# Hybrid decoder layer: attention scores, GLA products and the gate product on plain float32, softmax for eight heads at once, x kept for the first units

## The chip, the cores and the metric

The kernel runs on one core of one Trainium2 chip. The metric is device time in microseconds (us) of one execution; the time before is the median of three runs. The engines of the core are PE (TensorE), DVE (VectorE), ACT (ScalarE), POOL (GpSimd) and SP (SyncE, which here only issues DMAs).

## The reference

One layer for 2048 prompt tokens and 8 x 8 decode tokens, model width 1024, all in float32. One projection of x gives the inputs of two branches, a sliding-window attention (8 heads of width 64 on 2 KV heads, window 128, learned sink per head, relative bias) and a gated linear attention (GLA, 4 heads, key width 128, value width 256, a recurrent state). Both are gated, projected, merged, projected again and layer-normalised with the residual:

```python
z = einsum('btd,dn->btn', x, w_in)
q, k, v, g_att, gq, gk, gv, g_gla, g_lr, r_att, r_gla = split(z)
s = einsum(q, k) * HEAD_DIM**-0.5 + rel_bias          # 128 queries x 256 keys per block
m = max(max(s), sink); p = exp(s - m)
o_att = einsum(p / (sum(p) + exp(sink - m)), v)
log_a = log_sigmoid(g_lr @ w_gk_up + b_gk) / 16       # the gate product, rank 16
# GLA, chunk by chunk, b = cumsum(log_a):
o = einsum(q*exp(b), S) + einsum(tril(einsum(q*exp(b), k*exp(-b))), v)
S = exp(b_last) * S + einsum(k*exp(b_last - b), v)
h_att = (o_att * silu(g_att)) @ w_pa; h_gla = (norm(o) * silu(g_gla)) @ w_pg
y = (sigmoid(r_att) * h_att + sigmoid(r_gla) * h_gla) @ w_o
x = layer_norm(ALPHA * x + y)
```

Outputs are the new x for both kinds of tokens, the last window of keys and values, and the GLA states.

## The kernel before

**Projections.** All large products go through eight passes (lines 298 to 304): one over the attention columns (5 column groups), three over the GLA columns, then w_pa, the two merge gates and w_pg (4 groups each). A pass uses a seven-product scheme for 2 x 2 blocks (Strassen's kind: 7 block products, `ORDER` at line 51, instead of 8). A **unit** is one of the seven products for one of three token stretches (`s`, two times 352 tokens each); a **group** is one unit for one column group of 128 output rows. Each group is, for each of four 128-row slices of the contraction, three matmuls of 128 x 128 by 128 x 352 on `float32r` operands (lines 1160 to 1162): every float32 operand is split into a high part (a copy to `float32r`, made by ACT in line 144) and a low part (the difference, made by DVE or POOL in line 145), and high x high, low x high and high x low are summed in PSUM. `split` does both. DVE adds the products up (lines 236 to 253), and finished columns go to DRAM.

**Order of the work.** PE's instructions are issued in the order written; the other engines' instructions are ordered by the scheduler of the framework, within each engine first in, first out on the chip. Between two groups the main loop calls `tick()`, which runs what has been hung up with `at(t, fn)` for that tick. So attention, GLA, the set-up of masks and biases and the block combinations all run as side work between projection groups, at hand-set ticks (one tick is one group). Transfers of SP's queue go in order too: loads of x for a unit are issued two or three units ahead (lines 1140 to 1142).

**Start.** The first unit loads its quarter of x in four pieces; every further unit of products 1, 2 and 3 loads its own 704 KB from x (`raw_x`, line 204). For products 7, 6, 5 and 4, sums of blocks of x are needed: `xload` and `xcombo` (lines 501 to 526) load all of x again, in twelve jobs at ticks 1 to 25, compute the low-rank gate input with small matmuls (line 512), form the sums on DVE (lines 371 to 374) and store them in `xc_d`. The gate input is stored as high and low part (`gl_d`, 64 rows).

**Attention** (lines 536 to 645) works on eight stretches of 256 tokens, two blocks of 128 queries in each, five ticks per block (`SB = 5`, line 768). Keys are loaded twice per KV head into both halves of the partitions and split (line 569); queries are split into the halves of two tiles, `qa` and `qb` (lines 582 to 585), so that one matmul with 128 rows of contraction covers both parts. A call of `att_scores` treats one KV head: for each of four heads two `float32r` matmuls of 256 columns (lines 598, 599), bias added by DVE (line 600), maximum (603), four exponentials on ACT with their sums (606), small steps on 4 columns (604, 607 to 610), four scalings on DVE (612). `att_trans` transposes the probabilities on PE (line 623), four and five ticks after the scores; `att_out` multiplies with the values on float32 operands (line 639).

**GLA** (lines 796 to 1061) takes each head's 2048 prompt tokens in steps of 128, in chunks of 256 tokens, with the 64 decode tokens at the end of the last chunk. Steps stand `ST` ticks apart, about 4.9 by the formula at its end; the four heads follow each other. Per chunk: the gate product (line 856, on 96 rows: both parts of the operands stacked), log-sigmoid, cumulated sums, exponentials, and the products with q and k (`gla_kq`, with a split of the query). Per step: `gla_v` (two transposes, a split of the values), `gla_a` (the score product on float32 at line 916, a transpose of the keys at 917, the causal mask, splits of both), `gla_b` (three times `mm3`, three `float32r` products of 256 columns each, lines 938 to 940; the state update at 957, the state's split; a norm on ACT and POOL) and `gla_c` (two transposes at 967, the gating product on DVE). `samp_a` and `samp_b` do the same for the decode tokens.

**End.** After the last pass come the w_o product (lines 1205 to 1207 and 1216 to 1219) and the layer norm.

Of the kernel before, what the change touches and what calls it, by code (L numbers as in the profile page):

```python
# [29 lines left out]
G = 4  # L30
# [25 lines left out]
def kernel(ctx, tc, io):  # L56
# [63 lines left out]
    gl_d = dram.tile([64, NT], F32, name="gl_d")  # L120
# [185 lines left out]
    units = [(q, i, s) for q in passes for i in ORDER for s in range(MS)]  # L306
# [14 lines left out]
    for n in range(0, len(units), MS):  # L321
        q, i, _ = units[n]
        for p in range(q.np):
            plan[max(n - MS + MS * p // q.np, -1)].append((n, q, i, p))
    raws, wts, xs, xp, parts = {}, {}, {}, {}, {}

    def issue_w(n):
        for u, q, i, p in plan.get(n, []):
            raws[u, p] = q.raw_w(i, p)

    def make_w(n):
        for u, q, i, p in plan.get(n, []):
            wts[u, p] = q.prep_w(i, p, raws.pop((u, p)))

    def issue_x(n):
        if n < len(units) and n not in xs and n not in xp:
# [8 lines left out]
    def issue_parts(g):  # L345
        if g < len(groups) and g not in parts:
# [3 lines left out]
    combos = {"x": deque((xT, xc_d, 4, k, s) for s in range(MS) for k in range(4)),  # L350
              "a": deque((ua_d, ac_d, 2, k, s) for s in range(MS) for k in range(2)),
              "u": deque((None, uc_d, 4, k, s) for k0 in (0, 2) for s in range(MS) for k in (k0, k0 + 1))}

    def combine_load(job):
# [7 lines left out]
        x1 = mt("xk", 2 * T, 7, name="x1") if src is xT else w4(name="x1")[:, :2 * T]  # L362
        x2 = w4(name="x2")[:, :2 * T]
# [22 lines left out]
    raws[0, 0] = q0.raw_w(1, 0)  # L386
    x0 = mtile("xb", F32, "xs")
    hl0 = [mtile("xb", F32R, n) for n in ("xh", "xl")]
    for k in range(4):
        ts = slice(k * T, (k + 1) * T)  # L390
        nc.sync.dma_start(x0[:, ts], xT[:, k, toks(0, 0)])
        if k == 0:
            wts[0, 0] = q0.prep_w(1, 0, raws.pop((0, 0)))
        split(hl0[0][:, ts], hl0[1][:, ts], x0[:, ts])
    xp[0] = hl0
    for p in range(1, 5):
        raws[0, p] = q0.raw_w(1, p)
        wts[0, p] = q0.prep_w(1, p, raws.pop((0, p)))
    plan[-1] = [e for e in plan[-1] if e[0] != 0]
    issue_x(1)  # L400
    issue_x(2)
    issue_w(-1)
    make_w(-1)
    issue_w(0)
# [5 lines left out]
    bsel = const.tile([P, NB], F32, name="bsel")  # L410
# [88 lines left out]
    cx = {}  # L499

    def xload():
        job = combos["x"].popleft()
        cx[job[4], job[3]] = combine_load(job)

    def xcombo(s, k, eng):

        x1, x2, dst, last = cx.pop((s, k))
# [6 lines left out]
        combine_do(x1, x2, dst, last, eng)  # L514
        if k == 3:
            ps = glp.pop(s)
            gh, gl = (w4(F32R, n)[:, :T] for n in ("glh", "gll"))
            split(gh, gl, ps[:, :T])
            for i, g_ in enumerate((gh, gl)):
                for j in range(4):  # L520
                    r0 = 32 * i + 16 * (j // 2)
                    nc.gpsimd.dma_start(gl_d[r0:r0 + 16, toks(s, j % 2)], g_[32 * j:32 * j + 16].bitcast(F32))
# [13 lines left out]
    def att_load(c):  # L536
# [5 lines left out]
        A["kl"], A["kd"] = ([mt("kz", W + AT, 7, F32R, n) for _ in range(2)] for n in ("kl", "kd"))  # L542
        for kv in range(2):
            for r in (slice(0, HD), slice(HD, P)):
                nc.sync.dma_start(A["kl"][kv][r, k0:].bitcast(F32),
                                  z_kv[kv * HD:(kv + 1) * HD, 0, t0 - W + k0:t0 + AT])
        A["vT"] = mt("vT", AT, 1)
        nc.sync.dma_start(A["vT"], z_kv[:, 1, t0:t0 + AT])
# [851 lines left out]
```

## Time and profile before

| | |
|---|---|
| median of three runs | 1988.36 us (1981.45 to 1990.43) |
| profiled execution | 1982.41 us |
| span of its trace | 1980.6 us |
| PE, DVE, ACT, POOL busy | 91%, 77%, 49%, 36% of the span |
| mean granted TensorE clock | 0.957 |
| DMA | 430.67 MB, mean 217 GB/s |

The profile is of one execution. A row of the groups gives line, engine, operation, out<-in, shape and count; after the bar the group's busy us, the mean ns of one, and the idle time of the engine just before them with what ended it. A row of the waits gives who waited for whom, the total us, the times, and the longest. A row of the timeline gives the start and the duration in us and, in brackets, the idle time before it; the ends of matmuls are modelled, so the step from one start to the next is the better price of a matmul. A row of the stages gives the busy us of each engine in a stretch of the span, the granted clock, the DMA share and GB/s.

### The profile page before, as it was taken

The page shows a single profiled execution, that of the slowest core. Times are in us where ns is not written, and L with a number is a line of the kernel's source. Part 1 is how long each engine was busy: PE and PEld are TensorE (multiplying, and loading weights), DVE is VectorE, ACT ScalarE, POOL GpSimd, SP SyncE. Part 2 cuts the span into 40 slices and gives each one's busy share as a digit, 9 for nine tenths or more (in the row PEclk, how much of TensorE's full clock was granted, in tenths as well). Part 3 has the DMA queues.
Part 4 walks back from the last instruction along what each step waited for, and adds up shares of the span by engine and source line. Part 5 has one row for each costly group of instructions (what it writes and reads, how often), then busy time and mean ns, then how long its engine had stood idle before and what let it go on. Part 6 is the DMA issues. An engine that isn't in the chain of part 4 may idle for free.

```text
span 1980.6 us, 31502 instructions
## 1 busy us (share of the span) xinstructions
PE 1794.6 (91%) x10771; PEld 1669.9 (84%) x10771; DVE 1532.7 (77%) x2872; ACT 978.5 (49%) x2139; POOL 716.5 (36%) x604
## 2 busy tenths in 40 slices
PE   8699997988899989889899898999988999989998
PEld 7589986867689988878898798988888999987886
DVE  5657669998996798767987878799768957866656
ACT  3143345645554655665677466676655653212100
POOL 2442153231235645545442224311445216541111
PEclk9799999999899989999999899999998999999999
DMA  9966764444556777554566787578786897797431
GB/s 352 334 226 193 224 201 161 138 142 137 180 176 184 258 249 229 170 183 147 176 193 213 233 278 233 180 246 281 252 286 228 294 327 268 237 309 243 162 118 54
DMA packets 286833, 430.67 MB, mean 217 GB/s; under 512 B 28093, under 2 KB 227573, under 8 KB 286656
## 3 DMA queue, kind: packets, MB, share of 16 engines
q1 hardware_dynamic: 284720, 426.35, 66.1%
q0 software_dynamic: 1856, 2.17, 0.4%
q8 instruction: 85, 1.39, 0.3%
q14 instruction: 76, 0.62, 0.1%
q10 hardware_dynamic: 96, 0.13, 0.0%
HBM read 306.80 MB, written 122.63 MB: 217 GB/s over the span
## 4 chain that ended last, share of the span: by engine, by line
PE 41%; DVE 25%; DMA 13%; ACT 8%; POOL 6%; issue 5%; SPq 1%; DVEq 0%; POOLq 0%; ACTq 0%
PE pd L1160 9%; PE pd L1161 9%; PE pd L1162 8%; PE pd L1207 3%; PE pd L1206 3%; PE pd L1205 3%; DVE wl L145 2%; DVE s L612 2%; ACT xh L144 2%; DVE xl L145 2%; DMA ws<-w_g 2%; DMA ws<-w_at 1%; DVE nm L603 1%; POOL a L243 1%; DVE s L600 1%
## 5 line engine op out<-in xcount | busy, mean ns | idle before, releaser
L1160 PE MATMUL pd<-xh,wh 128*128 128x352 f32 x2484 | 842.3, 339 | 39.2 <-ACT xh L144 20.7
L1161 PE MATMUL pd<-xl,wh 128*128 128x352 f32 x2484 | 817.9, 329 | 20.1 <-DVE xl L145 14.8
L1162 PE MATMUL pd<-xh,wl 128*128 128x352 f32 x2484 | 816.2, 329 | 0.0
L1160 PEld LDWEIGHTS pd<-xh,wh 128*128 128x128 f32 x2484 | 482.6, 194 | 67.7 <-issue 22.8
L1161 PEld LDWEIGHTS pd<-xl,wh 128*128 128x128 f32 x2484 | 484.1, 195 | 23.9 <-DVE xl L145 17.7
L1162 PEld LDWEIGHTS pd<-xh,wl 128*128 128x128 f32 x2484 | 482.4, 194 | 0.0
L145 POOL TENSOR_TENSOR xl<-xs,xh 128x1408 fp32r<-128x1408 f32 x63 | 207.8, 3298 | 234.0 <-ACT xh L144 227.2
L144 ACT CAST xh<-xs 128x1408 fp32r<-128x1408 f32 (+2 forms) x171 | 218.2, 1277 | 109.5 <-PE pd L1161 93.6
L145 DVE TENSOR_TENSOR wl<-ws,wh 128x512 fp32r<-128x512 f32 (+1 forms) x231 | 190.9, 835 | 71.7 <-ACT wh L144 59.5
L145 DVE TENSOR_TENSOR xl<-xs,xh 128x1408 fp32r<-128x1408 f32 (+2 forms) x108 | 170.5, 1580 | 46.7 <-ACT xh L144 45.6
L144 ACT CAST wh<-ws 128x512 fp32r<-128x512 f32 (+1 forms) x231 | 134.7, 594 | 86.3 <-PE pd L1161 53.0
L243 POOL TENSOR_TENSOR a<-a,a 128x352 f32<-128x352 f32 x99 | 108.3, 1104 | 98.9 <-DVE a L242 93.4
L931 POOL TENSOR_SCALAR sq<-sq 128x1 f32<-128x1 f32 (+1 forms) x68 | 32.3, 476 | 260.6 <-ACT ring L930 260.6
L1205 PE MATMUL pd<-woh,x 128*128 128x512 f32 x256 | 101.2, 395 | 0.7 <-ACT woh L144 0.7
L1207 PE MATMUL pd<-wol,x 128*128 128x512 f32 x256 | 101.2, 395 | 0.6 <-DVE wol L145 0.6
L1206 PE MATMUL pd<-woh,x 128*128 128x512 f32 x256 | 101.4, 396 | 0.3 <-DVE x L145 0.3
L176 POOL TENSOR_TENSOR ws<-ws 128x512 f32<-128x512 f32 (+1 forms) x32 | 41.7, 1304 | 154.0 <-DVE fin L270 27.9
L606 ACT ACTIVATE s<-s,nm 128x256 f32<-128x256 f32 (+1 forms) x128 | 62.7, 491 | 58.5 <-DVE nm L604 57.6
L144 ACT CAST x<-xst 128x384 fp32r<-128x384 f32 (+2 forms) x48 | 22.3, 486 | 139.2 <-PE pd L1206 106.4
L933 ACT ACTIVATE ring<-pa,sq 128x256 f32<-128x256 f32 (+1 forms) x68 | 32.3, 474 | 118.0 <-POOL sq L932 118.0
L178 POOL TENSOR_TENSOR ws<-ws 128x512 f32<-128x512 f32 (+1 forms) x32 | 44.3, 1384 | 88.6 <-DMA ws<-w_g 30.0
L623 PE MATMUL pa<-ident,s 128*128 128x128 f32 x248 | 44.1, 307 | 35.5 <-DVE s L612 35.3
(284 smaller groups left out, 3354.7 us busy)
## 6 DMA issues: line engine op xcount, KB each, us to landing
xs<-xc_d SPq DMA_DIRECT2D x72, 704.0 KB, 4.6
xs<-xT SPq DMA_DIRECT2D x53, 704.0 KB, 4.6
ws<-w_g SPq DMA_DIRECT2D x108, 256.0 KB, 3.7
xc<-tt_d SPq DMA_DIRECT2D x48, 352.0 KB, 5.2
ws<-w_at SPq DMA_DIRECT2D x45, 256.0 KB, 6.4
ws<-w_ra SPq DMA_DIRECT2D x36, 256.0 KB, 4.3
ws<-w_rg SPq DMA_DIRECT2D x36, 256.0 KB, 4.5
ws<-w_pg SPq DMA_DIRECT2D x36, 256.0 KB, 4.8
```

Of the source, the lines that this page charges most:

```text
L144: pin["a"] = nc.scalar.copy(dst_h, src)
L145: i = eng.tensor_tensor(dst_l, src, dst_h.bitcast(F32), ALU.subtract)
L178: tt(r[0], r[0], r[1], ALU.add)
L243: pin["p"] = nc.gpsimd.tensor_tensor(u, u, a, ALU.add)
L606: nc.scalar.activation(s[:, g, k0:], s[:, g, k0:], AF.Exp, bias=nm[:, g:g + 1], accum_out=sm[:, g:g + 1])
L623: nc.tensor.transpose(tp[:, g * P:(g + 1) * P], s[:, g, hf * W:(hf + 1) * W], ident)
L1160: mm(ps, wh[:, ks], xh[:, ts], start=(k == 0), stop=False)
L1161: mm(ps, wh[:, ks], xl[:, ts], start=False, stop=False)
L1162: mm(ps, wl[:, ks], xh[:, ts], start=False, stop=(k == q.kh - 1))
L1205: mm(ps, xh[:, xs], hi, start=(k == 0), stop=False)
L1206: mm(ps, xl[:, xs], hi, start=False, stop=False)
L1207: mm(ps, xh[:, xs], lo, start=False, stop=(k == KT - 1))
```

## The change

- **Attention.** Keys and values are loaded once per stretch, unsplit; there are no split queries. Scores are single float32 matmuls with 64 rows of contraction, the two KV heads in rows 0 to 63 and 64 to 127 of the array; the scale moves into the bias step. One call takes two heads of each KV head, and the second call then does the softmax for all eight heads, with half of the scalings on ACT. A block has seven ticks; the transposes come five and six ticks after the second score call.
- **GLA.** All products are single float32 matmuls; the splits of query, values, scores, keys and state are gone. The transpose of the keys moves from `gla_a` to `gla_v`, and one ACT copy brings values and keys out of PSUM. The gate product has 32 rows instead of 96, and the gate input is stored without a low part. Within a step of `st` ticks, `gla_v` stands at a quarter, `gla_b` at three quarters, `gla_c` at one and a half. Attention ends 32 ticks later, so `ST` becomes about 4.4.
- **Decode tokens.** The GLA products use two row halves of the array; the old states are loaded five ticks ahead by a function of their own; the attention part's outputs are written from SP's queue instead of POOL's.
- **Start.** The first six units run as products 1 and 2 of one token stretch after the other. All eight row slices of x of a stretch are loaded once and kept: the units split from them, and the block sums are formed in place. Weights for the second unit are loaded right behind those of the first; the weights of the third product are all prepared in one unit, those of the fourth in two.

```diff
-    units = [(q, i, s) for q in passes for i in ORDER for s in range(MS)]
+    units = [(passes[0], i, s) for s in range(MS) for i in ORDER[:2]]
+    units += [(passes[0], i, s) for i in ORDER[2:] for s in range(MS)]
+    units += [(q, i, s) for q in passes[1:] for i in ORDER for s in range(MS)]
...
-            plan[max(n - MS + MS * p // q.np, -1)].append((n, q, i, p))
+            if n == 3 * MS:
+                plan[n - 2 + 2 * p // q.np].append((q, i, p))
+            elif n > 2 * MS:
+                plan[n - MS + MS * p // q.np].append((q, i, p))
+            elif n == 2 * MS:
+                plan[n - 1].append((q, i, p))
...
     def make_x(n):
-        if n < len(units) and n not in xp:
+        if n < 2 * MS and n not in xp:
+            _, i, s = units[n]
+            xp[n] = [mtile("xb", F32R, m) for m in ("xh", "xl")]
+            for k in range(4):
+                split(*(t[:, k * T:(k + 1) * T] for t in xp[n]), xk[s, k][i - 1][:, :T])
+        elif n < len(units) and n not in xp:
...
+    def xload(s, k, parts_=((0, 2), (1, 2))):
+        if (s, k) not in xk:
+            xk[s, k] = mt("xk", 2 * T, 7, name="x1"), w4(name="x2")[:, :2 * T]
+        for j, m in parts_:
+            o = 0 if m else 1
+            nc.sync.dma_start(xk[s, k][j][:, o * T:max(m, 1) * T if m else 2 * T],
+                              xT[:, 4 * j + k, 2 * s * T + o * T:2 * s * T + (m or 2) * T])
...
-    for j in range(12):
-        at(1 + 1.5 * j, xload)
-        at(8 + 1.5 * j, lambda j=j: xcombo(j // 4, j % 4, nc.vector))
+    for s in range(MS):
+        for k in range(4):
+            at(10 * s + min(2 + k, 4), lambda s=s, k=k: xcombo(s, k))
...
+    def att_scores(c, bi, g0):
...
+        ps = [pa().rearrange("p (a k) -> p a k", a=2) for _ in range(2)]
+        for j in range(2):
+            for kv in range(2):
+                r = slice(kv * HD, (kv + 1) * HD)
+                mm(ps[kv][:, j, k0:], A["zq"][r, g0 + j, qs], A["kk"][r, 0, ks], start=True, stop=True,
+                   tile_position=(kv * HD, 0))
+        for kv in range(2):
+            nc.vector.scalar_tensor_tensor(A["s", bi, kv][:, g0:g0 + 2, k0:], ps[kv][:, :, k0:], HD ** -0.5,
+                                           st1["bias", kv][:, g0:g0 + 2, k0:], ALU.mult, ALU.add)
+        if g0 == 0:
+            return
...
+        for h in range(NH):
+            sl = A["s", bi, h // G][:, h % G, k0:]
+            if h % 2:
+                nc.scalar.mul(sl, sl, rd[:, h:h + 1])
+            else:
+                nc.vector.tensor_scalar(sl, sl, rd[:, h:h + 1], None, op0=ALU.mult)
...
-    SB = 5
+    SB = 7
...
+            at(o + 1, lambda c=c, bi=bi: att_scores(c, bi, 2))
+            at(o + 6, lambda c=c, bi=bi: att_trans(c, bi, 0))
+            at(o + 7, lambda c=c, bi=bi: att_trans(c, bi, 1))
+            at(o + 9, lambda c=c, bi=bi: att_out(c, bi))
...
     def gla_v(B, i):
...
-        split(gh[:n], gl[:n], v)
+        nc.tensor.transpose(tp[:n, HV:HV + HK], B["k2"][:, ts], ident)
+        nc.scalar.copy(g[:n], tp[:n, :HV + HK])
...
     def gla_b(B, i):
...
-            mm3(op[:, :HV], [t[:, ts] for t in B["qi"]], R["Ss"][S], True, False)
+            mm(op[:, :HV], B["qb"][:, ts], R["S"][S], start=True, stop=False)
         sp = pa()
-        mm3(sp[:, :HV], kT2, gv, True, True)
-        mm3(op[:, :HV], As, gv, S is None, True)
+        mm(sp[:, :HV], kT2, gv, start=True, stop=True)
+        mm(op[:, :HV], As, gv, start=(S is None), stop=True)
...
-        if not (B["last"] and i == B["nt"] - 1):
-            split(R["Ss"][Sn][0], R["Ss"][Sn][1], R["S"][Sn])
...
-                at(o + 3, lambda B=B, i=i: gla_b(B, i))
-                at(o + 7, lambda B=B, i=i: gla_c(B, i, P, i * P))
+                at(o + st / 4, lambda B=B, i=i: gla_v(B, i))
+                at(o + 3 * st / 4, lambda B=B, i=i: gla_b(B, i))
+                at(o + 3 * st / 2, lambda B=B, i=i: gla_c(B, i, P, i * P))
```

More of the change, by code (lines that the diff above doesn't have):

```diff
@@ L497, with xcombo @@
     glp = {}
[L499 to L507, printed above, removed]
+    def xcombo(s, k):
+        x1, x2 = xk[s, k]
         if k == 0:
@@ L513, in xcombo @@
                stop=(k == 3), tile_position=(0, 32 * j))
-        combine_do(x1, x2, dst, last, eng)
+        combine_do(x1, x2, xc_d[:, :, s, k], (id(xc_d), s) if k == 3 else None, nc.vector)
+        if s + 1 < MS:
+            xload(s + 1, k)
         if k == 3:
             ps = glp.pop(s)
[L517 to L522, printed above, removed]
-    for j in range(12):
-        at(1 + 1.5 * j, xload)
-        at(8 + 1.5 * j, lambda j=j: xcombo(j // 4, j % 4, nc.vector))
+            g_ = w4(name="glh")[:, :T]
+            nc.scalar.copy(g_, ps[:, :T])
+            for j in range(4):
+                r0 = 16 * (j // 2)
+                nc.gpsimd.dma_start(gl_d[r0:r0 + 16, toks(s, j % 2)], g_[32 * j:32 * j + 16])
+    for s in range(MS):
+        for k in range(4):
+            at(10 * s + min(2 + k, 4), lambda s=s, k=k: xcombo(s, k))
     t0 = 30
@@ L564, in att_prep @@
         A = AS[c]
-        ks = slice(A["k0"], W + AT)
-        for kv in range(2):
-            kd, kl = A["kd"][kv][:, ks], A["kl"][kv][:, ks]
-            nc.scalar.copy(kd, kl.bitcast(F32))
-            nc.vector.tensor_tensor(kl, kl.bitcast(F32), kd.bitcast(F32), ALU.subtract)
         tp = pa()
         for i in range(AT // W):
-            nc.tensor.transpose(tp[:, i * P:(i + 1) * P], A["vT"][:, i * P:(i + 1) * P], ident)
+            nc.tensor.transpose(tp[:, i * P:(i + 1) * P], A["kk"][:, 1, (i + 1) * P:(i + 2) * P], ident)
@@ L817, in unit @@
     def unit(dt=F32, name="u"):
[L818 removed]
+        return mt("u", GU, 10, dt, name)
     def pair(name):
@@ L823, in gla_w @@
     def gla_w(h):
[L824 to L828 removed]
+        w = mt("wgk", HK, 2)[:32]
+        nc.sync.dma_start(w, io["w_gk"][:, h * HK:(h + 1) * HK])
         R["wgk"] = w
@@ L893, in gla_kq @@
             nc.vector.scalar_tensor_tensor(t[:, :n], zq[:, :n], HK ** -0.5, t[:, :n], ALU.mult, ALU.mult)
-        B["qi"] = unit(F32R, "qih"), unit(F32R, "qil")
-        split(B["qi"][0][:, :Tp], B["qi"][1][:, :Tp], B["qb"][:, :Tp])
     def gla_v(B, i):
@@ L973, in gla_store, with samp_state @@
         wrote(ug_d[B["h"]], 0, slice(B["t0"], B["t0"] + B["T"]))
+    def samp_state(B):
+        for bh in (0, 4):
+            S0 = w4(name="S0").rearrange("p (b v) -> p b v", b=4)
+            nc.sync.dma_start(S0, io["state"][bh:bh + 4, B["h"]].rearrange("b k v -> k b v"))
+            B["S0", bh] = S0
     def samp_a(B):
@@ L1145 @@
         make_w(n)
+        if n == 0:
+            for p in range(5):
+                wts[q0, 2, p] = q0.prep_w(2, p, raws.pop((q0, 2, p)))
         xh, xl = xp.pop(n)
```

258 lines of the change are left out of this document (92 added, 166 removed).

## The prediction

> **What bounds the kernel now.** The page comes first: its span and the busy time of the engines.
>
> ```profile
> span 1980.6 us, 31502 instructions
> PE 1794.6 (91%) x10771; PEld 1669.9 (84%) x10771; DVE 1532.7 (77%) x2872; ACT 978.5 (49%) x2139; POOL 716.5 (36%) x604
> ```
>
> PE at 91% says little by itself, since ends of matmuls are modelled and a waiting or slowly clocked PE can still look busy. So the second view cuts the span into stages: start (0 to 120 us), rest of the first projection (to 280), attention (to 610), GLA with the other projections (to 1600), and the end. Columns are the stage's us, then busy us (and instructions) of PE, PE's weight loads, DVE, ACT and POOL, then the granted clock, the DMA share and GB/s.
>
> ```profile
> 0.00:120.00 120.00, 93.58 (x541) 79.89 (x541) 70.08 (x106) 37.70 (x63) 42.69 (x66) 0.89 0.92 327
> 120.00:280.00 160.00, 156.05 (x952) 153.85 (x953) 102.39 (x151) 57.64 (x93) 50.67 (x34) 0.98 0.68 216
> 280.00:610.00 330.00, 288.06 (x1768) 249.66 (x1767) 302.93 (x601) 183.00 (x503) 114.06 (x67) 0.94 0.49 153
> 610.00:1600.00 990.00, 894.21 (x5609) 861.97 (x5608) 801.69 (x1636) 613.47 (x1347) 390.59 (x341) 0.96 0.71 228
> ```
>
> DVE is busy 92% of attention, 81% of the GLA stage and only 64% of the quiet stretch from 120 to 280. The start is full on the DMA side (0.92). How much of each stage is projection? The same view for line L1161 alone counts one product in three:
>
> ```profile
> 0.00:120.00 120.00, 51.64 (x148) 30.42 (x148) 0.89 0.92 327
> 120.00:280.00 160.00, 100.67 (x310) 59.26 (x310) 0.98 0.68 216
> 280.00:610.00 330.00, 113.94 (x348) 67.77 (x347) 0.94 0.49 153
> 610.00:1600.00 990.00, 474.85 (x1442) 281.49 (x1441) 0.96 0.71 228
> ```
>
> The price of a product is the step between starts, from the timeline of PE, where the second number is only the modelled duration:
>
> ```profile
> 566.67 0.32 PE L1161 MATMUL pd<-xl,wh 128*128 128x352 f32 x1
> 566.83 0.33 PE L1162 MATMUL pd<-xh,wl 128*128 128x352 f32 x1
> ...
> 568.43 0.28 PE L598 MATMUL pa<-kd,qb 128*128 128x256 f32 x1
> ...
> 569.39 0.33 PE L1160 MATMUL pd<-xh,wh 128*128 128x352 f32 x1
> ...
> 571.14 0.32 PE L1162 MATMUL pd<-xh,wl 128*128 128x352 f32 x1
> 571.40 1.94 PE L639 MATMUL pa<-pT,vt 128*64 128x512 f32 x8
> 573.26 0.43 PE L1160 MATMUL pd<-xh,wh 128*128 128x352 f32 x1
> ...
> 578.06 1.46 PE L623 MATMUL pa<-ident,s 128*128 128x128 f32 x8 [0.72 <-DVE s L612]
> 579.28 0.41 PE L1160 MATMUL pd<-xh,wh 128*128 128x352 f32 x1
> ```
>
> A projection product takes 0.16 us, a group of twelve 1.92. Projections therefore fill 148 x 3 x 0.16 = 71 us of the start, 149 of the next 160, 167 of attention's 330 and 692 of GLA's 990. The eight score products take 0.96 us (568.43 to 569.39), so 0.12 each; eight transposes 1.22; eight weighted-value instructions 1.86. Attention has 32, 31 and 15.5 such bursts: 31 + 38 + 29 = 98 us. What is left of its 330 is 65 us, 20%.
>
> For GLA one more piece of the timeline:
>
> ```profile
> 1005.10 0.38 PE L916 MATMUL pa<-dm,em 128*128 128x128 f32 x2
> 1005.32 0.27 PE L917 MATMUL pa<-ident,ek 128*128 128x128 f32 x1
> 1005.65 0.38 PE L856 MATMUL pa<-gin,wgk 96*128 96x256 f32 x1
> 1005.87 0.33 PE L1160 MATMUL pd<-xh,wh 128*128 128x352 f32 x1
> ```
>
> The nine products of a step have the scores' form (256 columns, split parts), so 9 x 0.12 = 1.08 us (six, 0.72, in each head's first): 68 us over 64 steps. L916 is one product on plain float32: it shows as two instructions, 0.22 us for 128 columns. With a transpose at 0.11 that gives 64 x 0.33 = 21; the other 256 transposes are 28; 36 gate products at 0.22 are 8. Left over are 990 - 692 - 125 = 173 us, 17%. So 7%, 17% and 20% of a stage are lost where DVE is 64%, 81% and 92% busy: the loss grows with DVE's load. The waits of PE, one row of attention, three of GLA and one of the start, say the same:
>
> ```profile
> PE pa L623 <- DVE s L612: 35.3, 20, 5.0
> ...
> PE pa L967 <- ACT ring L933: 14.9, 8, 4.2
> PE pa L938 <- ACT ak L144: 10.5, 9, 2.9
> PE pa L940 <- DVE ak L145: 10.5, 10, 2.0
> ...
> PE pd L1160 <- ACT xh L144: 15.6, 5, 5.8
> ```
>
> PE takes its instructions in written order, so a transpose that waits for a softmax holds all projections behind it. The bound is thus PE's in-order stream, lengthened by about 65 + 173 us of waits and slow clock that DVE and ACT cause, and in the start by loads of x.
>
> **The change, part by part. PE gets more work.** A 256-column product on float32 should take twice L916's 0.22, an estimate of 0.43. A GLA step has three where it had nine split ones: 1.29 against 1.08, +0.21 x 60, and 0.86 against 0.72 in four: +13 us. The scores become four float32 products, each on 64 rows of the array, the two KV heads in different halves. The nearest row for this is L639, which uses column halves: eight instructions of 512 columns in 1.86 us are four slots of 0.43, so both halves do run at once, plus 0.15, and its first starts 0.26 after the product before instead of 0.16. That is 0.25 us for changing the array's shape. Scores then take 4 x 0.215 + 0.25 = 1.11 us against 0.96: +5 us over 32. If row halves do not run together it is 8 x 0.215 + 0.25 = 1.97, +32; with no cost of the shape it is -3. I take +5, by the row it is nearest to. The gate product on 32 rows takes 0.43 + 0.25 against 0.22: +17 over 36, or +8 without the shape's cost; I take 17, for the same reason. Together +35 us.
>
> The Trainium skill speaks against this part: "TensorEngine Tiling (Array Packing)", Key Properties, says that changing the tiling mode drains TensorE. The 0.26 for 0.16 agrees, and the price here is from the rows, as the page gives none; without it the sum would be some 17 us lower. The same section says that different tiles work in parallel; for row halves no run so far shows it.
>
> **DVE and ACT lose work.** These are DVE's groups in attention, then in GLA:
>
> ```profile
> L612 DVE TENSOR_SCALAR s<-s,rd 128x256 f32<-128x256 f32 x120 | 56.6, 533 | 0.5
> L584 DVE SCALAR_TENSOR_TENSOR qa<-zq,qa 64x256 fp32r<-64x256 f32 x27 | 15.5, 576 | 0.8
> L585 DVE SCALAR_TENSOR_TENSOR qb<-zq,qb 64x256 fp32r<-64x256 f32 x27 | 11.4, 421 | 0.8
> L569 DVE TENSOR_TENSOR kl<-kl,kd 128x384 fp32r<-128x384 f32 x13 | 10.8, 831 | 0.3 <-ACT kd L568 0.3
> ...
> L145 DVE TENSOR_TENSOR ak<-aper,ak 128x128 fp32r<-128x128 f32 x64 | 34.0, 531 | 5.4 <-ACT ak L144 4.9
> L145 DVE TENSOR_TENSOR st<-ring,st 128x256 fp32r<-128x256 f32 x60 | 30.3, 505 | 10.2 <-ACT st L144 9.6
> L145 DVE TENSOR_TENSOR gv<-pa,gv 128x256 fp32r<-128x256 f32 x64 | 26.6, 416 | 18.4 <-ACT gv L144 18.0
> L145 DVE TENSOR_TENSOR qil<-gb,qih 128x256 fp32r<-128x256 f32 x28 | 22.3, 797 | 9.8 <-ACT qih L144 9.8
> ```
>
> In attention the splits of keys and queries go (10.8 + 15.5 + 11.4), half of the scaling moves to ACT (28), and the small steps run once for eight heads: at least 66 of 303 us. In GLA the four groups shown go, 113 of 802. Either stage comes to about 70% DVE. Between 64% and 81%, with 7% and 17% lost, that is some 10.5%. GLA: 104 of 990 instead of 173, so -69, and the decode state, loaded earlier, makes it -72. Attention: 35 of 330 would be -30; I take -25, because the softmax chain gets longer (below). ACT gives up the copies in front of those splits and gets 64 scalings and a wider copy per GLA step; at 183 of 330 us and 613 of 990 it has room. The attention steps are spread over seven groups instead of five per block, GLA steps stand 4.4 groups apart instead of 4.9; that moves work between stages and is free as long as neither fills DVE again. The normalised output is fetched 3.3 groups (6.3 us) after the step instead of 4 (7.7): the 14.9 us of L967 stay.
>
> **The start** loads each part of x for the first six units once. Six loads of this group go (the first in four pieces):
>
> ```profile
> xs<-xT SPq DMA_DIRECT2D x53, 704.0 KB, 4.6
> ```
>
> 6 x 704 KB are 4.3 MB; at 327 GB/s that is 13 us. The wait of 15.6 us is part of what it can come out of. The clock of 0.89 over 120 us is 13 us not granted, of which a third should return: -18 us in all. Bounds: -5, if the new order (both halves of x and two sets of weights before the second unit) starves that unit, and -30. Twenty output DMAs of the decode part move from POOL's to SP's queue, in front of the loads of x that are queued there; these run two to three units (eight to ten us each) ahead, which covers a short block. If that cover is gone, it costs a few us once: nothing in the sum. Fewer DMAs for the gate input are off the path too.
>
> **The sum:** +35 - 25 - 72 - 18 = -80 us. The profiled execution took 1982.4 us (span 1980.6 and 1.8 around it), 6 us under the median of the runs, 1988.4. I put the change on the median: 1908 us.
>
> **The rivals.** First, **slower by the eight-head chain.** Today's chain for four heads, from the timeline:
>
> ```profile
> 447.10 1.21 DVE L603 TENSOR_REDUCE nm<-s 128x4 f32<-128x1024 f32 x1
> 448.85 0.51 ACT L606 ACTIVATE s<-s,nm 128x256 f32<-128x256 f32 x1 [7.08 <-DVE nm L604]
> 452.63 1.13 DVE L612 TENSOR_SCALAR s<-s,rd 128x256 f32<-128x256 f32 x4
> ```
>
> Maximum to scaling is 453.76 - 447.10 = 6.7 us. Eight heads add a second maximum (1.2) and four exponentials (at 0.5, 2.0): 9.9, and two bias steps in front, about 11. The transposes now come five groups after the last scores, 9.6 us and one burst of 1.86 between: 11.5. It just fits, and with L612's mean of 533 ns the four scalings of 1.13 us take 2.1. My sum leaves 40 us of loss in attention, 2.5 per block. Over 7.5 us per block, a chain of 19, the whole gain is gone; at 22 us the loss is 10.5 x 16 = 168 instead of 40, and the time 1908 + 128 = 2036. For it speaks that every projection waits behind it; against it that DVE loses a quarter of its attention work.
>
> Second, **little gain:** waits follow the order of steps and not DVE's load. Then attention gives nothing, GLA the 21 us of its two ak rows and some 10 more, the start 15, PE costs 35: -11, so 1977.
>
> Third, **a large gain:** the loss falls to the 7% of the quiet stretch. Attention 23 (-42), GLA 69 (-104), start -25, PE +18 as the shape costs nothing: -153, so 1835. For it speaks the clock: attention and GLA were not granted 6% of 330 and 4% of 990, 60 us, and short waits may end that.
>
> That the change does not do what it says is excluded for the products and splits, which are in the code; for the row halves it is the +32 above (1935).
>
> **How the numbers follow.** Forecast 0.60 (1870 to 1945, the row-half case in it), large gain 0.15, little gain 0.14, slower 0.11. A measurement tells 0.5%, 10 us, from no change: under 1978 is faster. The little gain lies at that edge, 0.08 faster and 0.06 same. So faster 0.83, same 0.06, slower 0.11. The range 1838 to 1978 leaves out the slower case, half of the large gain's lower side and a little at the edge.
>
> **What would show it.** In the profile after: DVE near 70% in both stages; no splits of ak, st, gv; GLA products stepping at 0.21 per instruction; score instructions of the two halves starting together; PE's wait for s below 25 us; first-projection loads of x gone and the start's clock above 0.93. Wrong would be: score instructions one after another, PE waiting for s longer than the 35.3 us, or a gain with DVE still over 80%.

## The result, and the profile after

The median went from 1988.53 us to 1927.77 us (1926.0 to 1930.8), a ratio of 0.970 [0.968, 0.973]: 61 us faster, where 80 were forecast. The profiled execution took 1930.8 us, 52 less than that of before; the accounts below are made on the two profiles. One execution each of the kernels of experiments 4 and 9 took several times as long as the others (8991.6 and 4674.4 us, the latter the profiled one, so that experiment 9 has no account by stages); the ratios leave them out, and without them the medians given there would be 1902.0 and 1969.8 us.

First the page of the kernel after: its span and the engines.

```profile
span 1929.0 us, 30434 instructions
PE 1803.9 (94%) x10619; PEld 1638.7 (85%) x10619; DVE 1334.9 (69%) x2372; ACT 921.6 (48%) x1882; POOL 693.3 (36%) x572
```

DVE has lost 198 us of work, PE is busy 9 us longer in a shorter span. The stages of the kernel after, cut where its own stages change (attention now ends near 650), with the columns as before:

```profile
0.00:120.00 120.00, 101.67 (x598) 86.78 (x599) 72.53 (x122) 43.95 (x86) 37.16 (x52) 0.96 0.86 294
120.00:267.00 147.00, 136.92 (x832) 134.64 (x831) 88.84 (x133) 45.63 (x68) 45.55 (x31) 0.97 0.65 207
267.00:650.00 383.00, 369.72 (x2370) 320.15 (x2370) 278.97 (x477) 210.20 (x538) 161.00 (x81) 0.99 0.59 186
650.00:1550.00 900.00, 839.77 (x4988) 780.35 (x4987) 643.18 (x1266) 539.30 (x1063) 336.85 (x314) 0.98 0.72 230
```

DVE is busy 73% of attention (279 of 383) and 71% of GLA: the 70% of the forecast. Of these four stages the granted clock is up in all but the quiet one, most in the start (0.89 to 0.96) and in attention (0.94 to 0.99). The price of PE's new instructions stands in the timeline, where the second number is again only the modelled duration:

```profile
304.99 1.14 PE L587 MATMUL pa<-kk,zq 64*128 64x256 f32 x8
306.05 0.43 PE L1126 MATMUL pd<-xh,wh 128*128 128x352 f32 x1
...
708.00 0.59 PE L921 MATMUL pa<-ring,gb 128*128 128x256 f32 x2
708.43 0.59 PE L923 MATMUL pa<-ak 128*128 128x256 f32 x2
708.86 0.59 PE L924 MATMUL pa<-ak,aper 128*128 128x256 f32 x2
709.39 0.69 PE L844 MATMUL pa<-gin,wgk 32*128 32x256 f32 x2
710.01 0.43 PE L1126 MATMUL pd<-xh,wh 128*128 128x352 f32 x1
```

A float32 product of 256 columns shows as two instructions and steps by 0.43 us (708.00, 708.43, 708.86). The four score products, eight instructions on two row halves, take 1.06 us up to the next projection; one after another they would take eight times 0.215, 1.72. In the raw records the two halves start 5 to 7 ns apart in 113 of the 128 pairs; the others belong to bursts in which the halves did not stay in step. The waits, one row of attention (270 to 600), three of GLA (650 to 1550) and two of the start (0 to 120), with the total, the times and the longest:

```profile
PE pa L621 <- DVE s L611: 3.9, 3, 2.6
...
PE pa L937 <- ACT ring L911: 17.2, 8, 4.7
PE pa L923 <- ACT ak L891: 14.1, 6, 3.8
PE pa L923 <- ACT gv L891: 7.2, 3, 3.7
...
PE pd L1126 <- ACT xh L144: 13.1, 5, 4.8
...
PE pd L1127 <- DVE xl L145: 1.0, 1, 1.0
```

The wait for the softmax fell from 35.3 us to 3.9. GLA's waits are another matter. All of them together fell, from 95 us (610 to 1600 before) to 60, since the rows for split operands are gone; but L937 (L967 before) waits longer than it did, and L923 waits 21.3 us in two rows for one ACT copy, of values and keys (`ak` and `gv` are its buffers). And the loads of x, 53 before:

```profile
xs<-xT SPq DMA_DIRECT2D x48, 704.0 KB
```

**Where the time went.** Windows cut at fixed times hold different work in the two kernels. So I took the start times of the same projection products in the traces, and from each stretch took off 0.16 us per product. What is left is side work and loss, the **excess**. The cuts are product 1260 (end of the first projection), 2532 or 2916 (end of attention at five or seven ticks a block), 6804 (end of GLA) and the last one, 7811:

| excess, us | first projection | attention | GLA | last passes |
|---|---|---|---|---|
| before | 48 | 174 | 295 | 10 |
| after | 46 | 141 | 270 | 20 |
| difference | -2 | -33 | -26 | +10 |

The sum is -51, the difference of the two profiles. It serves for all experiments below.

### The profile page after: what moved, and what is told of

Same layout as the page of the kernel before. It is cut to its first block, busy times and chain, and to the rows that moved or that the text cites. A ratio compares the mean times of both kernels' runs of the same rounds, so it can differ in the third digit from the quotient of the medians.

```text
span 1929.0 us, 30434 instructions
## 1 busy us (share of the span) xinstructions
PE 1803.9 (94%) x10619; PEld 1638.7 (85%) x10619; DVE 1334.9 (69%) x2372; ACT 921.6 (48%) x1882; POOL 693.3 (36%) x572
## 4 chain that ended last, share of the span: by engine, by line
PE 56%; DVE 11%; DMA 10%; ACT 7%; POOL 5%; issue 4%; SPq 1%; DVEq 0%; POOLq 0%; ACTq 0%
PE pd L1126 12%; PE pd L1127 12%; PE pd L1128 11%; PE pd L1173 3%; PE pd L1172 3%; PE pd L1171 3%; DMA ws<-w_g 2%; POOL xl L145 1%; PE pa L587 1%; DVE wl L145 1%; PE pa L621 1%; PE pa L637 1%; DMA x<-ug_d 1%; PE pa L923 1%; DVE xl L145 1%
## 5 line engine op out<-in xcount | busy, mean ns | idle before, releaser
L1126 PE MATMUL pd<-xh,wh 128*128 128x352 f32 x2484 | 854.6, 344 | 35.6 <-ACT xh L144 13.1
L1126 PEld LDWEIGHTS pd<-xh,wh 128*128 128x128 f32 x2484 | 476.4, 192 | 85.9 <-issue 32.5
L1127 PEld LDWEIGHTS pd<-xl,wh 128*128 128x128 f32 x2484 | 479.1, 193 | 21.7 <-POOL xl L145 13.2
L1128 PEld LDWEIGHTS pd<-xh,wl 128*128 128x128 f32 x2484 | 475.4, 191 | 0.4 <-DVE wl L145 0.4
L144 ACT CAST xh<-xs 128x1408 fp32r<-128x1408 f32 (+1 forms) x162 | 208.8, 1290 | 115.7 <-PE pd L1127 101.7
L145 DVE TENSOR_TENSOR wl<-ws,wh 128x512 fp32r<-128x512 f32 (+1 forms) x231 | 200.0, 876 | 62.8 <-ACT wh L144 62.7
L145 DVE TENSOR_TENSOR xl<-xs,xh 128x1408 fp32r<-128x1408 f32 (+1 forms) x99 | 157.8, 1594 | 51.5 <-ACT xh L144 50.6
L911 ACT ACTIVATE ring<-pa,sq 128x256 f32<-128x256 f32 (+1 forms) x68 | 32.3, 474 | 168.7 <-POOL sq L910 168.7
L178 POOL TENSOR_TENSOR ws<-ws 128x512 f32<-128x512 f32 (+1 forms) x32 | 43.9, 1373 | 152.0 <-DMA ws<-w_pg 36.7
L176 POOL TENSOR_TENSOR ws<-ws 128x512 f32<-128x512 f32 (+1 forms) x32 | 42.3, 1323 | 140.0 <-DVE xl L145 39.5
L182 POOL TENSOR_TENSOR ws<-ws 128x512 f32<-128x512 f32 (+1 forms) x32 | 49.6, 1559 | 86.3 <-DMA ws<-w_pa 17.5
```

Source lines behind the costliest of these rows:

```text
L144: pin["a"] = nc.scalar.copy(dst_h, src)
L145: i = eng.tensor_tensor(dst_l, src, dst_h.bitcast(F32), ALU.subtract)
L178: tt(r[0], r[0], r[1], ALU.add)
L182: tt(r[0], r[0], A.pop((p, "s2")), ALU.subtract)
L1126: mm(ps, wh[:, ks], xh[:, ts], start=(k == 0), stop=False)
L1127: mm(ps, wh[:, ks], xl[:, ts], start=False, stop=False)
```

## The experiments

My first theory was the prediction's: the loss goes with DVE's load, in attention and in GLA. The rival: GLA's loss is the order of waits on ACT and POOL, whatever DVE has to do. "Before" beside a time is the kernel before, run on the same chip.

**1. DVE's work put back in attention.** The kernel after, with the subtractions of the removed key and query splits, written to a tile that nobody reads.

```diff
+        scr = mt("scr", W + AT, 1)
+        for _ in range(2):
+            nc.vector.tensor_tensor(scr[:, A["k0"]:], A["kk"][:, 0, A["k0"]:], A["kk"][:, 1, A["k0"]:], ALU.subtract)
+        for g in range(G):
+            for r in (slice(0, HD), slice(HD, P)):
+                nc.vector.scalar_tensor_tensor(scr[r, :AT], A["zq"][r, g], HD ** -0.5, A["zq"][r, g], ALU.mult, ALU.subtract)
```

> The changed kernel with DVE work put back in attention without anyone waiting for it: per stretch of 256 tokens two subtractions of 128 x 384 and eight of 64 x 256, the sizes of the removed splits of keys and queries, into a scratch tile: some 38 us of DVE work, all at the head of a stretch. The output is unchanged. Load theory: attention's DVE share goes from 73% to about 82% and the loss grows from 7% to some 17%: 20 to 35 us more, 1948 to 1963. Rival (the batched softmax and the wider spacing made the gain, the splits did not matter): under 10 us more.

1962.3 us (before 1988.7), ratio 0.987 [0.983, 0.991]: 35 us slower than after, for 49 us more of DVE (1384.2 busy against 1334.9). This kernel's PE wait in attention:

```profile
PE pa L627 <- DVE s L617: 30.5, 9, 7.3
```

Work whose result nobody needs brings the softmax wait back, from 3.9 to 30.5 us. The excess of attention goes from 141 to 175 us, all other stages stay within 4. The time lies in the theory's range. But the added operations did not only work, they also waited, at the head of DVE's queue, for the load of the queries:

```profile
DVE scr L578 <- DMA zq<-z_q: 20.0, 5, 5.1
```

The first softmax wait of PE behind each of these five places comes 9 to 15 us later, and these five make 22.8 of the 30.5 us. So DVE operations of the removed sizes are enough to bring attention's loss back; whether by their busy time or by the queue that they hold up, no run tells.

**2. The same in GLA.** The kernel after, with DVE subtractions of the sizes of the removed splits of query, values, keys, scores and state.

```diff
+        nc.vector.tensor_tensor(R["scr"][:, :Tp], B["qb"][:, :Tp], rmask[:, :Tp], ALU.subtract)
...
+        nc.vector.tensor_tensor(R["scr"][:n], g[:n, :HV], rmask[:n], ALU.subtract)
+        nc.vector.tensor_tensor(R["scr"][:n, :P], g[:n, HV:], rmask[:n, :P], ALU.subtract)
...
+        nc.vector.tensor_tensor(R["scr"][:, :P], A_, rmask[:, :P], ALU.subtract)
...
+        nc.vector.tensor_tensor(R["scr"], R["S"][Sn], rmask, ALU.subtract)
```

> The changed kernel with DVE's work in GLA put back without anyone waiting for it: per step four subtractions of the sizes of the removed splits (256, 128, 128 and 256 columns) and one of 256 per chunk, written to a scratch tile. The output is unchanged. Load theory: DVE is back at about 81% in the GLA stage and the stage loses 40 to 70 us more: 1968 to 1998. Rival (GLA's loss is set by chains through ACT and POOL and their distances, not by DVE's load): at most 15 us more, 1928 to 1943.

1950.9 us (before 1988.7), 0.981 [0.977, 0.985]: 23 us slower than after, for 107 us more of DVE. Its GLA stage, columns as above:

```profile
650.00:1550.00 900.00, 823.98 (x4828) 761.77 (x4826) 737.51 (x1545) 530.37 (x1047) 338.60 (x307) 0.97 0.70 223
```

DVE is back at 82% there (81% before), and GLA's excess rises by 27 us. One us of DVE costs 0.2 in GLA, where the added operations waited for ACT's copies for 14 us, and 0.7 in attention, its waits included. The result lies between theory and rival: DVE's load is a part of GLA's loss, not its rule.

**3. ACT's copies put back in GLA.** The kernel after, with ACT copies of those sizes at the same places.

```diff
+        nc.scalar.copy(R["scr"][:, :Tp], B["qb"][:, :Tp])
...
+        nc.scalar.copy(R["scr"][:n], g[:n, :HV])
+        nc.scalar.copy(R["scr"][:n, :P], g[:n, HV:])
...
+        nc.scalar.copy(R["scr"][:, :P], A_)
...
+        nc.scalar.copy(R["scr"], R["S"][Sn])
```

> The changed kernel with ACT work put back in GLA without anyone waiting for it: per step four copies of the sizes of the removed splits, one per chunk, to a scratch tile (some 85 us of ACT time). The output is unchanged. If GLA is bound by chains through ACT (norm, gate exponentials, the copy of values and keys), it costs more than the same work on DVE did (23 us): 1958 to 1985. If ACT has room, under 10 us: 1928 to 1938.

1937.9 us (before 1988.0), 0.975 [0.973, 0.977]: 10 us slower than after, for 80 us more ACT work in the GLA stage (619 against 539), at the upper edge of the second expectation. The amount of ACT's work is not the bound either.

**4. ACT never waits for POOL.** What does ACT wait for? Its group for the last step of GLA's norm in the kernel after (after the bar: busy, mean ns of one, idle before it and what ended it), and POOL's groups around it, all from 650 to 1550:

```profile
L911 ACT ACTIVATE ring<-pa,sq 128x256 f32<-128x256 f32 (+1 forms) x68 | 32.3, 474 | 168.7 <-POOL sq L910 168.7
```

```profile
L145 POOL TENSOR_TENSOR xl<-xs,xh 128x1408 fp32r<-128x1408 f32 x28 | 92.9, 3317 | 83.0 <-ACT xh L144 70.1 <-PE pa L899 7.1 <-PE pa L937 3.9
...
L910 POOL TENSOR_TENSOR sq<-sq,mhalf 128x1 f32<-128x1 f32 (+1 forms) x68 | 41.1, 604 | 5.5
L909 POOL TENSOR_SCALAR sq<-sq 128x1 f32<-128x1 f32 (+1 forms) x68 | 28.6, 421 | 185.2 <-ACT ring L908 185.2
```

ACT squares the output, POOL turns the sum into a factor (two small steps, 1.0 us, sometimes behind a subtraction of 3.3), and ACT waits 2.5 us on average before it scales. Behind it in ACT's queue stand the copies of values and keys, for which PE waits at L923. In the trace, before each of the nine waits of L923 ACT had stood at L911 for 1.9 to 9.3 us; 4 to 11 us lie between L911 and the copy, filled mostly with the chunk's gate work, in which two instructions ACT_TABLE_LOAD take 1.28 us each. Before the change, the same group waited 118.0 us (L933). The experiment lets ACT copy the output unscaled, and POOL applies the factor to the copy:

```diff
-        nc.scalar.activation(on[:n], o, AF.Square, scale=1.0 / 16, accum_out=sq[:n])
+        nc.scalar.activation(R["scr"][:n], o, AF.Square, scale=1.0 / 16, accum_out=sq[:n])
+        nc.scalar.copy(on[:n], o)
...
-        nc.scalar.mul(on[:n], o, sq[:n])
+        nc.gpsimd.tensor_scalar(on[:n], on[:n], sq[:n], None, op0=ALU.mult)
```

> The changed kernel with ACT freed from waiting inside GLA's norm: ACT takes the sum of squares into a scratch tile, copies the output unscaled, and POOL, which computes the factor, also applies it (one more POOL operation of 128 x 256 per step). In the changed kernel ACT stood 159 us in the GLA stage in front of the scaling, waiting for POOL, with everything behind it in its queue. Theory (this blocked queue is what keeps GLA's loss up): 1890 to 1912 and PE's waits for the copy of values and keys mostly gone. Rival (ACT has idle time anyway, and POOL's longer chain delays the transposes of the output): 1923 to 1945.

1903.4 us (before 1984.7), 0.957 [0.954, 0.961]: 24 us faster than after. Its waits in GLA (650 to 1530), PE's and then the largest of ACT's:

```profile
PE pa L939 <- POOL ring L913: 26.1, 13, 4.9
PE pa L925 <- ACT ak L892: 4.4, 3, 1.7
...
ACT scr L909 <- PE pa L926: 47.6, 37, 5.3
```

This tells more than the time. The output transposes (L939) wait longer than after (26.1 for 17.2), since the output is ready later; yet GLA's excess falls from 270 to 241. What fell is the wait for the copies behind ACT's blocked place (14.1 and 7.2 to 4.4 us in all), and of ACT's 168.7 us at that place nothing is left (its waits for POOL are 11 us in all). So the blocked queue was worth 24 us. ACT stood there before the change too; what that cost was not tried. The edit also frees the output's place in PSUM without POOL, but this can explain little: PE's waits on L911 at lines other than L937 were 1.8 us in the kernel after (L899 and L980).

**5. Values fetched earlier.** The kernel after, with `gla_v` a tick before its step.

```diff
-                at(o + st / 4, lambda B=B, i=i: gla_v(B, i))
+                at(o - 1, lambda B=B, i=i: gla_v(B, i))
```

> The changed kernel with the transposes of values and keys one tick before the step's score product instead of a quarter step after it, so that ACT's copy has about two ticks (4 us) more before its first reader. If PE's waits for that copy (21 us in the GLA stage, and more that show as a wait of the weight load) are what GLA lost, 1900 to 1912. If the wait only moves to the next thing in ACT's queue, 1920 to 1930.

1915.2 us (before 1984.7), 0.964 [0.960, 0.967]: 13 us faster than after, between the two expectations; GLA's excess 260. Where the copy has more time, the blocked queue costs less.

**6. The gate product without the change of the array's shape.** The kernel after, its gate product on 128 rows: its 32 input rows loaded four times, the weights repeated to match and scaled by a quarter.

```diff
-        w = mt("wgk", HK, 2)[:32]
+        w = mt("wgk", HK, 2)
+        nc.vector.tensor_scalar(w, w, 0.25, None, op0=ALU.mult)
...
-        g = B["gin"] = unit(name="gin")[:32]
-        nc.sync.dma_start(g[:, :T_], gl_d[:, t0:t0 + T_])
+        g = B["gin"] = unit(name="gin")
+        for r in range(4):
+            nc.sync.dma_start(g[32 * r:32 * r + 32, :T_], gl_d[:, t0:t0 + T_])
```

> The changed kernel with the gate product on all 128 rows: four copies of the 32 input rows (three more small loads per chunk) and weights at a quarter. The array keeps its shape. If the change of shape costs what the trace suggests (0.82 us per gate product against 0.43 for the product itself), 36 of them give 10 to 14 us: 1914 to 1919. If the cost is the product's, 1924 to 1932.

1927.2 us (before 1988.0), 0.970 [0.968, 0.972]: no difference to after. Yet a GLA step with a gate product, up to the second projection product behind it, went from 2.12 to 1.73 us (medians), 14 us over 36. GLA's excess fell by only 5 us, to 265, so 10 of the 14 came back as loss. One row of its waits grew, 14.1 in the kernel after:

```profile
PE pa L925 <- ACT ak L893: 20.0, 10, 4.3
```

The row for the same copy in its other buffer grew as well (7.2 to 9.6), but that for the output fell (L939, 17.2 to 11.3). So the rows do not tell where all of the saving went.

**7. Those three together**, with `gla_c` moved from 3/2 to 15/8 of a step so that the norm on POOL has time.

```diff
-                at(o + 3 * st / 2, lambda B=B, i=i: gla_c(B, i, P, i * P))
+                at(o + 15 * st / 8, lambda B=B, i=i: gla_c(B, i, P, i * P))
```

> The changed kernel with four edits together: the norm's scaling on POOL, values and keys transposed one tick before the step, the output fetched at 15/8 of a step instead of 3/2, and the gate product on 128 rows. If GLA's waits are taken away by the first three, the 14 us of PE time that the gate on 128 rows saves arrive at the end as well: 1865 to 1895. If the waits only move, 1910 to 1930.

1885.5 us (before 1984.7), 0.949 [0.946, 0.952]: 42 us under after, and the fastest of all. The counts of one projection product in three from 650 to 1530, of the kernel after, of the fourth experiment and of this one:

```profile
650.00:1530.00 880.00, 413.48 (x1269) 244.44 (x1268) 0.98 0.72 230
```

```profile
650.00:1530.00 880.00, 425.24 (x1312) 251.09 (x1312) 0.98 0.74 237
```

```profile
650.00:1530.00 880.00, 436.31 (x1341) 256.88 (x1341) 0.98 0.77 247
```

In the same 880 us, 43 and 72 more such products come through; three at 0.16 us each, that is 21 and 35 us (in both kernels GLA ends before 1530, so the windows hold a little of the last passes). GLA's excess is 231 us, 10 under that of experiment 4. With bursts priced as in the next section, side work is 169 us for 178 there and the loss 63 in both. As far as these two traces tell, what came on top of experiment 4 is most of the gate product's saving; the earlier values took no further loss away. No run has the other edits without the gate's, and the three single gains (24, 13 and 0) already make 37 of the 42 us. Its wait for the output transposes is down to

```profile
PE pa L941 <- POOL ring L915: 6.2, 2, 4.8
```

**8 to 10. One part alone on the kernel before**: the start (units, `xload`, weights), the attention part with its spacing of seven ticks, the GLA part with the gate at the old spacing of 4.9. Each edit is that part of the change; the line that tells it:

```diff
 start      +    units = [(passes[0], i, s) for s in range(MS) for i in ORDER[:2]]
 attention  +                mm(ps[kv][:, j, k0:], A["zq"][r, g0 + j, qs], A["kk"][r, 0, ks], start=True, stop=True,
 GLA        +        mm(sp[:, :HV], kT2, gv, start=True, stop=True)
```

> The kernel before with the start part of the change alone (order of the first six units, x loaded once and kept, weights of the second product loaded early). The prediction's step says 18 us less, about 1970. The two traces say that some 9 us are won by the 30th group and most of it is lost again by the end of the first projection: 1983 to 1988.

> The kernel before with the attention part of the change alone (unsplit keys and queries, scores on row halves, softmax for eight heads, seven ticks per block). Spacing alone made the kernel before 35 us slower, of which some 30 us are in the GLA steps that come to stand closer together. Load theory for attention: its stage gains some 35 to 50 us as in the changed kernel, and GLA, still with all its splits, gives back 25 to 40: 1965 to 1995. Rival (attention's gain stands by itself and GLA's steps do not mind the 4.4 ticks once attention is light): 1940 to 1955.

> The kernel before with the GLA part of the change alone (float32 products, no splits, quarter-tile steps, 32-row gate product), at the old spacing of 4.9 ticks since attention stays. If the DVE and ACT work taken off GLA is worth what it cost to put back (23 us for DVE), minus some 35 to 45 us of added PE time, the result is within 20 us of before: 1975 to 2005. If quarter-tile steps themselves free PE, under 1965.

| part alone | us (before) | ratio |
|---|---|---|
| start | 1981.0 (1988.7) | 0.995 [0.993, 0.997] |
| attention | 1971.1 (1988.0) | 0.991 [0.989, 0.993] |
| GLA | 1973.0 (1988.0) | 0.993 [0.991, 0.996] |

That is -8, -17 and -15, in sum -40, where the whole change brings -61. The attention part lies in its first range; the start (1981.0) and the GLA part (1973.0) each miss both of theirs by 2 us or more and lie between. The excess of the start part alone falls by 10 us in the first projection and changes by 1 or less in every other stage; that of the GLA part by 12 in GLA and 5 in the first projection, and rises by 7 in the last passes. The first stage of the start part alone:

```profile
0.00:120.00 120.00, 102.99 (x602) 88.11 (x602) 73.87 (x126) 44.92 (x87) 44.91 (x67) 0.94 0.88 304
```

**11. The spacing alone on the kernel before.**

```diff
-    SB = 5
+    SB = 7
```

> The kernel before with one number changed: seven ticks per attention block instead of five; scores, splits and softmax stay as before. Load theory (a stage loses time as DVE fills up, so the gain in attention comes from the work taken off DVE): attention keeps all its DVE work, the GLA steps move closer together, and the total stays within 10 us of before, 1978 to 1998. Rival (the gain comes from the wider spacing alone): most of the some 50 us that attention gained appears here, 1940 to 1955.

2024.0 us (before 1988.7), 1.017 [1.014, 1.021]: 35 us slower, outside both expectations. The old attention stage and GLA of this kernel:

```profile
280.00:610.00 330.00, 279.95 (x1634) 248.96 (x1633) 278.28 (x516) 166.31 (x434) 118.26 (x56) 0.93 0.50 156
610.00:1600.00 990.00, 879.91 (x5498) 838.24 (x5497) 796.71 (x1654) 613.35 (x1377) 374.66 (x341) 0.95 0.68 215
```

DVE's share in attention is lower (278 for 303 us of 330), and by the rule of the prediction the lost share had to fall. It rose: attention's excess went from 174 to 197 us, and with bursts priced as in the next section the loss went from 17% of the stage to 21%. GLA's excess went from 295 to 315.

**12. The old spacing in the kernel after.**

```diff
-    SB = 7
+    SB = 5
```

> The changed kernel with the attention blocks five ticks apart instead of seven; all else, the transposes' five and six ticks included, stays, and the GLA steps go back to about 4.9 ticks from 4.4 by their formula. Theory: closer GLA steps are what the wider attention spacing costs (alone, in the kernel before, it made the time 35 us longer), so giving it back brings GLA 20 to 35 us, and attention, with about 70 us less DVE work than before, loses less than 10: 1895 to 1915 us against 1928, with PE's wait for s in attention below 15 us. Rival: the softmax for eight heads needs the seven ticks, since two blocks' chains now overlap on DVE: PE's wait for s comes back above 25 us and the time is 1930 to 1965 us.

1942.0 us (before 1990.0), 0.977 [0.975, 0.979]: 14 us slower than after. Theory and rival both fall, though the rival named a range that holds the time. PE's wait for the softmax does not come back; the largest row for s in attention is

```profile
PE pa L587 <- DVE s L590: 5.4, 5, 3.1
```

and attention's excess is 139 us at five ticks, 141 at seven. It is GLA that lost: 286 against 270, at steps 4.9 ticks apart instead of 4.4. So the new GLA steps run 16 us better at 4.4, and the old ones (experiment 11) 19 us worse. That bears on the difference of the sums (21 us) as well: the attention part alone should pay those 19 us in old GLA steps (-33 + 19 = -14; -17 measured, not split by stages), and the GLA part alone stands at 4.9, where it has 12 of the 26 us. The two amounts together are more than the 21 us, and the start goes the other way (-8 alone, -2 in the whole), so the parts do not simply add up. Steps hung up at fractions of a tick run at whole ticks, so another spacing is also another order; whether that is how 4.4 differs from 4.9 was not tried.

## Why the prediction was right, and where not

The sign, the size and the range were right; some 20 us of the sum were not. Part of this is luck: against the forecast of the parts, attention brought 13 us more, while GLA and the start brought 16 less each and the last passes cost 10 that were not forecast, so the misses partly cancel.

- **PE's prices** were right. A 256-column float32 product was put at 0.43 us and takes 0.43; a score burst at 1.11 and takes 1.06. If each kind of burst is priced by its cheap occurrences (the tenth in a hundred, up to the second projection product behind it), GLA's side work goes from 146 to 178 us: +33, where +30 was forecast (13 + 17). Only the gate product was somewhat low: put at 0.68 in place of 0.22, it takes 0.82 us where it stands alone (0.12 before) and 0.61 at the cheapest inside a step.
- **Row halves run together.** The Trainium skill, "TensorEngine Tiling (Array Packing)", Key Properties, says that different tiles work in parallel; the trace agrees for row halves, with starts 5 to 7 ns apart. The rival price of +32 us (1935) asked for 1.97 us per burst where 1.06 were measured, so it falls.
- **Attention** was put at -25 and +5, and came to -33. The place of the gain was right: the first experiment takes back the whole of it with operations on DVE alone. That it is DVE's load is not shown, since most of the softmax wait came back behind places where DVE stood waiting for a load. The size was cautious, as I had charged 5 us of loss to the longer chain for eight heads; PE's wait for s was 3.9 us, not the 25 that I allowed.
- **GLA** was put at -72 and +30, and came to -26: with 33 of PE work, the loss fell by 58, from 149 to 91 us. The forecast of 10.5% loss at 70% DVE came out (91 of 892 us, 10.2%), but by luck: the step behind it, "the loss grows with DVE's load", failed here. With DVE at 82% again, the second experiment loses 27 us, not 58; ACT's copies add 10. The other 20 or so came with the removed instructions and the new order, not with the load; which of them was not tried. What remains of the loss is in good part a queue: ACT stood 169 us waiting for POOL, and without that the kernel is 24 us faster. The prediction saw this wait as "the 14.9 us of L967 stay": it read what PE waits for by name, not what stands behind the waiting instruction on ACT.
- **The line through three stages** (7%, 17% and 20% lost at 64%, 81% and 92% DVE) had a low end that was not DVE's. The only wait of PE between 120 and 280 us in the kernel before is for POOL:

```profile
PE pd L1161 <- POOL xl L145: 4.0, 1, 4.0
```

  It and the half clock behind it (from 265.8 to 272.6 us in the raw records, 3.4 us) are most of the 11 us that the prediction took as the loss of the quiet stretch.
- **The start** was put at -18, and came to -2. By the 30th group 9 us were won and the clock stood at 0.96, as forecast. Alone, the part keeps this (-10 in its trace, -8 in the medians). In the whole change 7 us are lost again between the 45th and the 75th group. PE's waits of the kernel after from 120 us to the end of the first projection are these, and neither the kernel before nor the start part or the GLA part alone has one in that stretch:

```profile
PE pd L1126 <- DVE a L247: 2.6, 1, 2.6
PE pd L1127 <- DVE xl L145: 1.6, 1, 1.6
```

  Behind them the clock is at 0.5 from 190.7 to 194.1 us, another 1.7 us. The wait of 15.6 us for the copy of x, out of which the gain was to come, is still 13.1; what fell in the first 120 us is the wait for the low part of x, from this row of the kernel before to 1.0 us:

```profile
PE pd L1161 <- DVE xl L145: 9.7, 4, 6.3
```

  What of the other parts brings the new waits on DVE was not tried.
- **The last passes** were put at nothing and cost 10 us more in this profile; the GLA part alone shows 7, and the other profiles on the kernel after 4 to 7. At two places PE now waits for DVE's sums of products (L253 and L236, 6.3 us together), rows that the kernel before does not have there. Why DVE is late there stays open.
- **The spacing** of seven ticks was called free as long as DVE is not full. It is free in the new attention (141 against 139). In the old one it cost 23 us at a lower DVE share: reading a stage's loss from DVE's share does not hold from one order of the work to another.

Of the rivals, the slower one (the eight-head chain, 2036) fell with the 3.9 us, and again in the last experiment, where five ticks suffice. The little gain (1977) was wrong in size, but its sentence, "waits follow the order of steps and not DVE's load", is nearer to what GLA showed, where DVE's load is worth 27 of the 58 us. The large gain (1835) asked for a loss of 7% in both stages; attention came to 9% (35 of 406 us, by the same pricing), GLA to 10%.

## What to carry to other kernels

A loss that goes with an engine's load in three stages of one trace is a correlation: put the load back as work that nobody waits for, stage by stage, before it becomes the price of a change, and see in the trace that the added work does not itself wait at the head of its queue. Where a list of waits names a copy on an engine with room, look at what that engine itself waits for: a small step that crosses to another engine and back blocks everything queued behind it. A saving on the bounding engine (here 14 us of the gate product, of which the time showed nothing alone) can come through once the waits next to it are gone, so try such edits together as well as alone.

## What the runs showed of the hardware

- Float32 matmuls show as two instructions each and step by 0.43 us for 256 columns, where a `float32r` product of 256 columns stood at 0.12: three float32 products cost a fifth more than nine split ones, and save the splits.
- A change of the array's shape for one product cost nearly as much as the product: alone between projections the gate product took 0.82 us on 32 rows and 0.43 on 128, with the same columns.
- Of DVE work added whose result nobody needs, 0.7 us of each us reached the end in attention, where it also stood 20 us waiting for loads, and 0.2 in GLA.
- A short wait of PE can cost more than itself. From the timeline of PE in the kernel before, in attention:

```profile
438.32 0.77 PE L623 MATMUL pa<-ident,s 128*128 128x128 f32 x5 [2.83 <-DVE s L612]
...
441.82 0.58 PE L598 MATMUL pa<-kd,qa 128*128 128x256 f32 x1 [2.26 <-ACT pT L627]
...
444.02 0.49 PE L1161 MATMUL pd<-xl,wh 128*128 128x352 f32 x1
444.31 0.49 PE L1162 MATMUL pd<-xh,wl 128*128 128x352 f32 x1
```

  And the granted clock there, in the third column from the end:

```profile
440.00:446.00 6.00, 4.18 (x15) 4.18 (x16) 5.13 (x11) 1.56 (x3) 0.00 (x0) 0.50 0.54 191
```

  Behind the second wait projection products step by 0.29 us instead of 0.16, until 446.4: twelve products lose 1.6 us beside the 2.26 of the wait. So the list of waits, in which the softmax's fell by 31 us, does not show all that such a wait costs; the granted clock of attention rose from 0.94 (of 330 us) to 0.99 (of 383 us) as well. In the records of the clock 19 and 5 us were not granted in these two stretches; so some 13 of attention's 33 us are the clock's.
